# A hybrid decoder step on one core: the instruction planner's prices for VectorE, ScalarE and GpSimd are set to durations from the profile

## The chip, the cores and the metric

One core of a Trainium2 chip runs the whole program. Its engines are TensorE (PE, matmuls; PEld is its weight load), VectorE (DVE), ScalarE (ACT), GpSimd (POOL) and SyncE (SP, which starts most DMAs). The metric is device microseconds of one execution. The kernel before takes 2442.61 us, the median of 3 runs (2437.9 to 2442.79).

## The reference

One inference step of four layers on 1024 prompt positions and 8 x 4 sample positions, all with the same weights, width 1024, all in float32. Each layer is `x <- LayerNorm(ALPHA * x + mixer(x))`; the mixers are a short gated convolution (A), native sparse attention (B), an RG-LRU (C) and the convolution again (A).

```python
# A: short gated convolution
h, b_gate, c_gate, z = split(x @ w_in, 4)
y = (silu(z) * b_gate * causal_dwconv(c_gate * h, buf, conv_w)) @ w_out

# B: three attentions over one projection, added with gates, then (o * silu(z)) @ w_out
k_c, v_c = einsum('bnjcgd,cjgd->bncgd', blocks_of_32_rows, w_cmp)   # compressed rows of the cache
p_c = masked_softmax(q @ k_c)                                        # compressed attention
idx = top_k(sums of p_c by block of 64, 16)                          # selected blocks
o = g0 * (p_c @ v_c) + g1 * attend(q, rows of blocks idx) + g2 * attend(q, last 512 rows)

# C: gated linear recurrence along time
a = exp(-8 * softplus(-lam) * sigmoid(uc @ w_a + b_a))
b = sqrt(1 - a * a) * sigmoid(uc @ w_x + b_x) * uc
h[t] = a[t] * h[t-1] + b[t]
y = (silu(z) * h) @ w_out
```

The sample group attends to 4096 past rows in a paged cache, which is read through a page table. Outputs are both activations and the new states and caches.

## The kernel before

**Tiles and stages.** Activations lie transposed, channels on partitions, in 8 tiles of 128 channels by 1056 columns (1024 prompt, 32 sample). A dense product takes three blocks of 352 columns; every operand is split into a high and a low part, so a product over 1024 channels is 24 matmuls of 352 columns into one PSUM bank (`dense`). The high part is written by ACT (or DVE), the low part by DVE or POOL (`split`). The stages follow each other: layer A with the compression of the sample cache beside it (`layer_a`, `compress`, to 432 us), its output product and norm (`out_phase`), the projections of layer B (`b_project`), the sample group's attention (`decode`, 690 to 856), the prompt's attention (`prompt_attention`, to 1470), the norm of B, layer C (`layer_c`, 1590 to 1832), its norm, the second A (to 2325) and the last output product and norm (`final_phase`).

**The compression.** For each of 64 units (8 groups of rows by 8 sequences) POOL starts a gather of 1 MB from the cache, POOL or DVE (odd or even sequence) multiplies 1024 elements a partition by the weights, and DVE adds 512, 256 and 256 elements. A unit is recorded every 1/0.7 dense products (`RATE`), and a gather waits for the sum three units before (`GAHEAD`). The weights of a group have a single buffer.

**What sets the order.** Nothing is issued in the order in which it is written. `Rec` stands in place of the engines: each call is recorded as a step with its engine, a price in ns (`cost`, line 269), the tiles it reads and writes, and a due number, which is its place in the program less a shift (`AHEAD`, `DSH`: tables by kind of work). Up to six matmuls into one tile make one step. At the end of a part, `lay` simulates the five engines: at each turn the engine that can go first takes, of the steps that are ready by then, the one with the smallest due number. A step is ready when its producers have ended and a latency between the two engines has passed (`LAT`, line 246: 205 ns from PE to DVE, 192 from DVE to ACT, 141 from ACT to DVE, 127 from DVE to DVE), and when its buffers are free; buffers of a ring are given out in recorded order (`admit`). A change of ACT's table costs 1283 ns, a DMA takes its bytes at 360 a ns on a bus of its own plus 2000 ns. The simulated times are then thrown away: what is kept is the order of the steps on every engine. On the chip each engine runs its queue in that order and waits at its head for what is not there. Since nearly all calls go through `add`, the profile shows line 307 for them; line 312 is the gather.

The prompt's attention has a planner of its own (`Plan`), whose steps carry literal prices, and which does not call `cost`.

Of the kernel before, what the change touches and what calls it, by code (L numbers as in the profile page):

```python
# [240 lines left out]
class Rec:  # L241
# [27 lines left out]
    def cost(self, eng, name, a, k, out):  # L269
        def free(v):  # L270
            return int(np.prod(v.shape[1:]))
        n = free(out)
        if eng == "PE":
            if name == "transpose":
                return 109
            m = a[2]
            return max(free(m) / 2.27 * (4 if m.dtype == F32 else 1), 50) + 7
        if eng == "ACT":
            ap = sum(1 for x in (k.get("bias"), k.get("scale")) if x is not None and not isinstance(x, (int, float)))
            src = a[1]  # L280
            return n * .833 + 51 + (0 if isinstance(src, View) and src.t.whole else 43) + 93 * ap + (93 if k.get("accum_out") is not None else 0)
        if eng == "DVE":
            if name == "reciprocal":
                return 6.25 * n + 69
            if name == "tensor_tensor_scan":
                return n * 2.08 + 70
            if name in ("tensor_reduce", "max"):
                n = free(k["in_"])
            return n / .96 + 70
        if eng == "POOL":  # L290
            if name == "tensor_scalar":
                return .833 * n + 327
            if name in ("tensor_copy", "memset"):
                return .833 * n + 150
            return 2.1 * n + 150
        return 0

    def add(self, eng, real, name, a, k):
# [11 lines left out]
    def gather(self, out, src, idx, **keys):  # L310
        def fn():
            self.nc.gpsimd.indirect_dma_start(out=out.real(), out_offset=None, in_=src, in_offset=bass.IndirectOffsetOnAxis(ap=idx.real(), axis=0))
        self.record("POOL", "gather", 1040, fn, [out], [idx], out, **keys)

    def record(self, eng, name, cost, fn, outs, ins, out, rk=(), wk=(), a=(), k={}):
        last = self.ops[-1] if self.ops else None
        if eng == "PE" and last is not None and last.eng == "PE" and last.out is outs[0].t and len(last.fns) < 6 and last.due - self.pos + self.shift > -1.5:
            o = last
            o.cost += cost
            o.fns.append(fn)  # L320
        else:
            o = Step()
            o.eng, o.cost, o.due, o.fns, o.deps, o.tiles, o.takes, o.outs = eng, cost, self.pos - self.shift, [fn], set(), {}, [], []
            o.weak, o.follow = set(), []
            o.func = a[2] if eng == "ACT" and name == "activation" and a[2] in (AF.Tanh, AF.Exp, AF.Sqrt) else None
            o.out = outs[0].t if outs else None
            o.size = int(np.prod(out.shape)) * 4 if eng == "SP" or name == "gather" else 0
            self.pos += 1
            self.ops.append(o)
# [1908 lines left out]
class Plan:  # L2238
# [10 lines left out]
    def add(self, kind, eng, cost, due, fn, r=(), w=(), after=()):  # L2249
        n = len(self.ops)  # L2250
        deps = set(after)
        for k in r:
            if k in self.wr:
                deps.add(self.wr[k])
        for k in w:
            if k in self.wr:
                deps.add(self.wr[k])
            deps.update(self.rd.get(k, ()))
        for k in r:
            self.rd.setdefault(k, []).append(n)  # L2260
        for k in w:
            self.wr[k], self.rd[k] = n, []
        self.ops.append([eng, cost, due + self.off.get(kind, 0.0), fn, sorted(deps)])
        return n
# [155 lines left out]
```

## Time and profile before

| | |
|---|---|
| median of 3 runs | 2442.61 us |
| profiled execution | 2450.34 us |
| its span | 2448.6 us |
| mean granted TensorE clock | 0.971 |
| PE busy | 2318.3 us (95%) |
| DVE busy | 1594.0 us (65%) |
| ACT busy | 1206.7 us (49%) |
| POOL busy | 955.4 us (39%) |
| HBM traffic | 237.31 MB read, 84.48 MB written |

All times are of one profiled execution. An engine's busy time is the union of its instructions' recorded durations; a recorded duration can lie partly beside the next one's. Waits are put down to the semaphore that came last. PE is busy nearly all the time, so what matters of another engine is whether PE waits for it.

### The profile page before, as it was taken

The page shows a single profiled execution, that of the slowest core. Times are in us where ns is not written, and L with a number is a line of the kernel's source. Part 1 is how long each engine was busy: PE and PEld are TensorE (multiplying, and loading weights), DVE is VectorE, ACT ScalarE, POOL GpSimd, SP SyncE. Part 2 cuts the span into 40 slices and gives each one's busy share as a digit, 9 for nine tenths or more (in the row PEclk, how much of TensorE's full clock was granted, in tenths as well). Part 3 has the DMA queues.
Part 4 walks back from the last instruction along what each step waited for, and adds up shares of the span by engine and source line. Part 5 has one row for each costly group of instructions (what it writes and reads, how often), then busy time and mean ns, then how long its engine had stood idle before and what let it go on. Part 6 is the DMA issues. An engine that isn't in the chain of part 4 may idle for free. (4 is left out here: it accounts for less than half of the span.)

```text
span 2448.6 us, 41435 instructions
## 1 busy us (share of the span) xinstructions
PE 2318.3 (95%) x14801; PEld 2247.7 (92%) x14801; DVE 1594.0 (65%) x3686; ACT 1206.7 (49%) x2761; POOL 955.4 (39%) x1070
## 2 busy tenths in 40 slices
PE   8999997998989999999999999899989899999996
PEld 8999986997979889999999989899889899999996
DVE  5777865584368767777777766877873743333336
ACT  3211211244357778888888862568872432222233
POOL 3455543223148656656555542323452320000131
PEclk9999998999999999999999999999989999999998
DMA  8999987256367641111112314421204221111111
GB/s 286 352 340 350 341 273 235 90 188 219 93 204 259 249 133 50 51 35 46 43 45 68 121 44 150 137 80 44 60 26 127 83 66 52 44 41 55 35 45 71
DMA packets 334643, 320.35 MB, mean 131 GB/s; under 512 B 19462, under 2 KB 301542, under 8 KB 324964
## 3 DMA queue, kind: packets, MB, share of 16 engines
q1 hardware_dynamic: 325220, 250.58, 33.1%
q0 software_dynamic: 9216, 67.11, 7.2%
q8 instruction: 117, 1.92, 0.3%
q14 instruction: 90, 0.74, 0.1%
HBM read 237.31 MB, written 84.48 MB: 131 GB/s over the span
## 5 line engine op out<-in xcount | busy, mean ns | idle before, releaser
L307 PE MATMUL mm<-x,w 128*128 128x352 f32 x5760 | 947.9, 326 | 23.2 <-DVE c L307 9.9
L307 PEld LDWEIGHTS mm<-x,w 128*128 128x128 f32 x5760 | 937.8, 191 | 28.3 <-DVE c L307 10.4
L307 PE MATMUL mm<-big,w 128*128 128x352 f32 x2208 | 389.0, 331 | 9.9 <-ACT c L307 5.5
L307 PEld LDWEIGHTS mm<-big,w 128*128 128x128 f32 x2208 | 366.3, 193 | 13.7 <-ACT c L307 6.9
L307 POOL TENSOR_TENSOR w<-ws,w 128x1024 fp32r<-128x1024 f32 (+1 forms) x43 | 105.8, 2461 | 446.7 <-ACT w L307 426.8
L1965 DVE TENSOR_TENSOR c<-T,c 128x512 fp32r<-128x512 f32 (+1 forms) x320 | 204.8, 648 | 49.6 <-ACT c L1961 44.8
L1961 ACT CAST c<-T 128x512 fp32r<-128x512 f32 (+1 forms) x320 | 174.6, 552 | 59.5 <-PE T L1957 38.4
L307 ACT CAST w<-ws 128x1024 fp32r<-128x1024 f32 (+2 forms) x116 | 120.4, 1039 | 158.0 <-PE mm L307 122.9
L638 PE MATMUL D<-x,w 128*128 128x352 f32 x1008 | 195.4, 330 | 2.3 <-DVE big L2092 2.3
L1867 PE MATMUL A<-big 128*128 128x320 f32 (+11 forms) x832 | 181.8, 334 | 3.6 <-DVE ast L1892 1.8
L1972 PE MATMUL O<-c,big 128*128 128x256 f32 x1056 | 180.4, 291 | 0.5 <-ACT c L1961 0.2
L307 ACT CAST big<-aux 128x352 fp32r<-128x352 f32 (+3 forms) x116 | 45.7, 400 | 268.6 <-DVE aux L307 251.0
L307 DVE TENSOR_TENSOR big<-big 128x256 f32<-128x256 f32 (+3 forms) x204 | 145.9, 730 | 39.0 <-POOL big L307 35.0
L638 PEld LDWEIGHTS D<-x,w 128*128 128x128 f32 x1008 | 159.9, 188 | 5.7 <-DVE big L2092 3.5
L307 DVE TENSOR_TENSOR w<-ws,w 128x1024 fp32r<-128x1024 f32 (+2 forms) x73 | 90.9, 1245 | 110.2 <-ACT w L307 109.6
L307 POOL TENSOR_TENSOR big<-big,ws 128x1024 f32<-128x1024 f32 (+1 forms) x38 | 89.8, 2364 | 154.5 <-DMA big<-in_cache_nsa_kv,idx 69.8
L1972 PEld LDWEIGHTS O<-c,big 128*128 128x128 f32 x1056 | 147.2, 189 | 2.6 <-DVE c L1965 0.7
L1925 POOL TENSOR_SCALAR pr<-pr,G,ast 128x32 f32<-128x32 f32 (+6 forms) x192 | 126.4, 675 | 47.1 <-DVE ast L1936 42.3
L1867 PEld LDWEIGHTS A<-big 128*128 128x128 f32 x832 | 134.3, 192 | 10.4 <-PE A L1867 2.3
L307 DVE SCALAR_TENSOR_TENSOR c<-c,mm 128x352 f32<-128x352 f32 x125 | 64.3, 516 | 108.6 <-PE mm L307 53.9
L307 ACT ACTIVATE aux<-ws,PT 128x352 f32<-128x352 f32 (+2 forms) x72 | 42.6, 594 | 173.1 <-DVE ws L307 171.8
L1921 ACT ACTIVATE pr<-pr,ast 128x32 f32<-128x32 f32 (+6 forms) x192 | 118.4, 619 | 18.2 <-DVE ast L1892 17.1
(286 smaller groups left out, 4047.2 us busy)
## 6 DMA issues: line engine op xcount, KB each, us to landing
ws<-in_a_w_in SPq DMA_DIRECT2D x64, 512.0 KB
raw<-big SPq DMA_DIRECT2D x128, 256.0 KB
big<-raw SPq DMA_DIRECT2D x128, 256.0 KB
c<-dd SPq DMA_DIRECT2D x48, 176.0 KB
xs<-x SPq DMA_DIRECT2D x24, 352.0 KB
x<-xs SPq DMA_DIRECT2D x8, 1056.0 KB
ws<-in_a_w_out SPq DMA_DIRECT2D x16, 512.0 KB
ws<-in_c_w_in SPq DMA_DIRECT2D x16, 512.0 KB
```

What stands on the lines that cost most here:

```text
L307: getattr(real, name)(*[f(x) for x in a], **{q: f(x) for q, x in k.items()})
L638: self.nc.tensor.matmul(ps, a, b, start=n == 0, stop=n == 23 and last)
L1867: nc.tensor.matmul(o, q[:, hl, i * P:(i + 1) * P], k, start=m == 0, stop=m == 1)
L1921: nc.scalar.activation(S[:, a:a + m], S[:, a:a + m], AF.Exp, bias=st[:, k:k + 1], scale=-1.0, accum_out=st[:, 3 + k:4 + k])
L1925: nc.gpsimd.tensor_scalar(S[:, a:a + m], S[:, a:a + m], G[:, i, 16 * k + h:16 * k + h + 1], st[:, 6 + k:7 + k], op0=ALU.mult, op1=ALU.mult)
L1961: nc.scalar.copy(x["H"][:, 0:n], x["tp"][:, 0:n])
L1965: nc.vector.tensor_sub(x["L"][:, 0:n], x["tp"][:, 0:n], x["H"][:, 0:n].bitcast(F32))
L1972: nc.tensor.matmul(O, v, M[:, y * P:(y + 2) * P], start=done[0] == 0, stop=done[0] == total - 1)
```

## The change

Prices in `Rec.cost` and in `gather`. ACT: the fixed part goes from 51 to 160 ns, the addition for a source in SBUF from 43 to 35, for each per-partition operand from 93 to 100, for an accumulator from 93 to 185. DVE: the fixed part from 70 to 150 ns; the scan from 2.08 to 2.6 ns an element; an instruction with two tensor inputs of which none is in PSUM gets 1.4 ns an element and 130 ns. POOL: two-input instructions from 2.1 ns an element and 150 ns to 2.25 and 170. The gather from 1040 to 1130 ns. PE's prices, `LAT`, the DMA prices and all other tables stay.

```diff
--- before.py
+++ after.py
@@ -278,21 +278,24 @@
         if eng == "ACT":
             ap = sum(1 for x in (k.get("bias"), k.get("scale")) if x is not None and not isinstance(x, (int, float)))
             src = a[1]
-            return n * .833 + 51 + (0 if isinstance(src, View) and src.t.whole else 43) + 93 * ap + (93 if k.get("accum_out") is not None else 0)
+            return n * .833 + 160 + (0 if isinstance(src, View) and src.t.whole else 35) + 100 * ap + (185 if k.get("accum_out") is not None else 0)
         if eng == "DVE":
             if name == "reciprocal":
                 return 6.25 * n + 69
             if name == "tensor_tensor_scan":
-                return n * 2.08 + 70
+                return n * 2.6 + 150
             if name in ("tensor_reduce", "max"):
                 n = free(k["in_"])
-            return n / .96 + 70
+            ins = [x for x in a[1:] + [k.get("in0"), k.get("in1")] if isinstance(x, View) and free(x) > 1]
+            if len(ins) > 1 and not any(x.t.ring.tag in ("mm", "aux") for x in ins):
+                return n * 1.4 + 130
+            return n / .96 + 150
         if eng == "POOL":
             if name == "tensor_scalar":
                 return .833 * n + 327
             if name in ("tensor_copy", "memset"):
                 return .833 * n + 150
-            return 2.1 * n + 150
+            return 2.25 * n + 170
         return 0
 
     def add(self, eng, real, name, a, k):
@@ -310,7 +313,7 @@
     def gather(self, out, src, idx, **keys):
         def fn():
             self.nc.gpsimd.indirect_dma_start(out=out.real(), out_offset=None, in_=src, in_offset=bass.IndirectOffsetOnAxis(ap=idx.real(), axis=0))
-        self.record("POOL", "gather", 1040, fn, [out], [idx], out, **keys)
+        self.record("POOL", "gather", 1130, fn, [out], [idx], out, **keys)
 
     def record(self, eng, name, cost, fn, outs, ins, out, rk=(), wk=(), a=(), k={}):
         last = self.ops[-1] if self.ops else None
```

## Rows read from the trace of the kernel before

**Rows 1.** The page, part 1: busy us (share of the span) xinstructions of each engine
```profile
PE 2318.3 (95%) x14801; PEld 2247.7 (92%) x14801; DVE 1594.0 (65%) x3686; ACT 1206.7 (49%) x2761; POOL 955.4 (39%) x1070
```

**Rows 2.** Busy time by stage: stretch, us, PE PEld DVE ACT POOL, PEclk, DMA
```profile
0.00:432.00 432.00, 394.76 (x2392) 387.12 (x2393) 298.76 (x495) 88.22 (x162) 194.08 (x117) 0.97 0.93 311
...
690.00:856.00 166.00, 153.34 (x1037) 137.43 (x1038) 132.50 (x331) 119.57 (x227) 116.67 (x106) 0.95 0.70 239
856.00:1470.00 614.00, 601.84 (x4309) 580.54 (x4308) 462.37 (x1425) 495.15 (x1412) 347.96 (x590) 0.98 0.22 64
...
1590.00:1832.00 242.00, 222.20 (x1342) 218.73 (x1343) 191.88 (x350) 185.38 (x313) 94.55 (x84) 0.97 0.18 52
...
1955.00:2325.00 370.00, 369.57 (x2283) 369.60 (x2284) 139.38 (x279) 86.89 (x153) 27.37 (x19) 0.99 0.18 51
```

**Rows 3.** PE's waits, 432:690 (9), 690:856, 1470:1955 (20), 2325:2449: us, times, longest
```profile
PE mm L307 <- ACT c L307: 5.3, 1, 5.3
...
PE aux L307 <- POOL c L307: 0.2, 1, 0.2
...
PE aux L307 <- DMA sel<-kcd: 8.1, 1, 8.1
...
PE aux L307 <- DVE SC L307: 7.8, 1, 7.8
...
PE mm L307 <- DVE w L307: 1.0, 1, 1.0
...
PE aux L307 <- DVE c L307: 4.6, 4, 2.4
```

**Rows 4.** Timeline of PE, four stretches of 0:432: start, us, [idle before <-releaser]
```profile
328.06 2.42 PE L307 MATMUL mm<-x,w 128*128 128x352 f32 x7 [6.01 <-DVE c L307]
...
372.73 1.53 PE L307 MATMUL mm<-x,w 128*128 128x352 f32 x6 [3.84 <-DVE c L307]
...
400.92 1.54 PE L307 MATMUL mm<-x,w 128*128 128x352 f32 x4 [3.25 <-DVE ws L307]
...
429.80 1.02 PE L307 MATMUL aux<-idf,SC 128*18 128x128 f32 x4 [11.34 <-DVE big L307]
```

**Rows 5.** Timeline of DVE ahead of those four waits
```profile
320.66 1.22 DVE L307 TENSOR_TENSOR big<-big,ws 128x1024 f32<-128x1024 f32 x1 [8.41 <-DMA ws<-in_b_w_cmp]
...
371.01 1.23 DVE L307 TENSOR_TENSOR big<-big,ws 128x1024 f32<-128x1024 f32 x1 [7.83 <-DMA ws<-in_b_w_cmp]
...
394.31 3.80 DVE L307 TENSOR_TENSOR big<-big 128x512 f32<-128x512 f32 x3 [8.34 <-POOL big L307]
...
423.67 2.81 DVE L307 TENSOR_TENSOR big<-big 128x512 f32<-128x512 f32 x1 [7.11 <-POOL big L307]
```

**Rows 6.** Timeline of 1503.5:1505: a chain DVE, ACT, DVE in a norm stage
```profile
1503.60 0.50 DVE L307 SCALAR_TENSOR_TENSOR c<-c,mm 128x352 f32<-128x352 f32 x1
...
1504.19 0.50 ACT L307 ACTIVATE c<-c 128x352 f32<-128x352 f32 x1 [1.34 <-DVE c L307]
...
1504.72 0.80 DVE L307 TENSOR_TENSOR big<-big,c 128x352 f32<-128x352 f32 x1 [0.61 <-ACT c L307]
```

**Rows 7.** Timeline of DVE, 1575:1577: six instructions that don't wait for each other
```profile
1575.27 1.26 DVE L307 TENSOR_SCALAR c<-idf,stat 128x128 f32<-128x128 f32 x6
```

**Rows 8.** Groups by shape: line engine op xcount | busy us, mean ns | idle before
```profile
L307 DVE SCALAR_TENSOR_TENSOR c<-c,mm 128x352 f32<-128x352 f32 x125 | 64.3, 516 | 108.6 <-PE mm L307 53.9 <-ACT c L307 52.4 <-issue 1.0
...
L312 POOL DMA_INDIRECT big<-in_cache_nsa_kv,idx x64 | 74.8, 1169 | 80.5 <-DVE idx L307 16.6 <-DMA raw<-big 16.5 <-DVE c L307 15.0
...
L307 DVE TENSOR_TENSOR big<-big 128x512 f32<-128x512 f32 x66 | 64.6, 980 | 36.2 <-POOL big L307 35.0 <-DMA ws<-in_a_w_in 1.0
...
L307 DVE TENSOR_TENSOR c<-c 128x352 f32<-128x352 f32 x77 | 50.7, 703 | 8.2 <-ACT c L307 8.2
...
L307 ACT COPY c<-mm 128x352 f32<-128x352 f32 x48 | 21.3, 455 | 34.2 <-PE mm L307 34.2
...
L307 POOL TENSOR_TENSOR c<-c 128x352 f32<-128x352 f32 x19 | 20.8, 1095 | 50.1 <-DVE c L307 22.6 <-ACT c L307 10.7 <-issue 8.8
...
L307 DVE TENSOR_SCALAR c<-idf,stat 128x128 f32<-128x128 f32 x54 | 11.8, 281 | 0.0
```

## The prediction

> **What bounds the kernel now.** I read five views in this order. The page first: TensorE (PE) is busy for 2318.3 us of a span of 2448.6 [rows 1], so about 130 us are all that any new order of instructions could return. The profiled execution took 2450.34 us; the median of the three runs shown is 2442.61, 0.3% less. I make the sum in differences and add them to the median; on the profiled execution the same differences stand.
>
> Then the busy time by stage [rows 2]. In the second short-convolution layer (1955 to 2325) PE is busy for 369.57 of 370 us: nothing to win, only to lose. In the prompt attention (856 to 1470) it is idle for 12.2 us, and that stage is ordered by `Plan`, which carries its own prices; the diff does not touch them. Attention is a quarter of the time and stays as it is, but for its start. What the change can move is the first layer with the cache compression beside it (0 to 432: PE idle 37.2 us), the decode attention (690 to 856: 12.7), the RG-LRU layer (1590 to 1832: 19.8), the norm stages between them and the tail.
>
> Then who ended PE's waits [rows 3], then the four long waits of the first layer one by one [rows 4], and what VectorE (DVE) did in them [rows 5]. Last come the durations themselves: a dependent chain of three instructions [rows 6], a burst of independent ones [rows 7], and the means of the groups that the new prices stand for [rows 8].
>
> **The change, part by part.** No instruction is added, removed or altered. Only numbers in `Rec.cost` and `gather` change, and these decide at which simulated moment an instruction is ready and its engine free; `lay` then takes the ready one with the smallest due number. Every queue is affected at once: ACT, DVE and POOL directly, PE in how it interleaves, the DMA starts by when buffers come free.
>
> *The size of the prices.* DVE with one operand in PSUM, 352 wide: 352/.96+70 = 437 ns before, 517 after; the trace says 516. DVE with two SBUF inputs: 437 before, 623 after, trace 703; for 512: 603 before, 847 after, trace 980. ACT copying 352 from PSUM: 344 before, 453 after, trace 455. POOL on two SBUF inputs: 889 before, 962 after, trace 1095. Gather: 1040 before, 1130 after, trace 1169 [rows 8]. So the change does what it says: the new prices are recorded durations, still short for POOL and SBUF pairs.
>
> *Durations are not occupancies.* Six independent tensor_scalars, 281 ns each by their group [rows 8], took 1.26 us together [rows 7]: (1.26-0.281)/5 = 196 ns from start to start. The old price is 128/.96+70 = 203, the new 283. The last 85 ns of a recorded duration lie beside the next instruction. The same tail is in `LAT`, which is left alone: in the chain of rows 6 the DVE instruction starts at 1503.60 and the ACT instruction that needs it at 1504.19, 0.59 us later; the old plan says 437+192 = 629 ns, the new one 517+192 = 709. From ACT to the next DVE instruction it is 0.53 us; old 293+51+43+141 = 528, new 293+160+35+141 = 629. So old prices and `LAT` fit a chain through PSUM and ACT, and the new plan believes each such hop 80 to 100 ns too long. Where two SBUF inputs meet, it is the other way: there the old plan is short by a third and the new one nearly right. I expect both errors to matter, in different stages.
>
> The Trainium skill has a rule against my reading of the burst: VectorE: DVE Perf Modes, section The DRAIN you can't avoid, says that the next instruction does not start until the pipe is empty. By it duration would be occupancy, the new prices would be right throughout, and my loss below would go. The trace disagrees (196 ns apart at 281 ns each), and the same section says that an instruction that is not held starts earlier.
>
> *First term, the first layer: a gain.* The four waits of rows 4 are 6.01, 3.84, 3.25 and 11.34 us, 24.4 together. Rows 5 show why: DVE stands for 7 to 8 us at the head of its queue before a product or a sum of the compression, and that stands behind a load or behind POOL, while the dense work that frees PE's banks is queued behind it. The plan had believed the compression ready some 8 us too early. With the new prices it becomes ready later in the plan: by 90 (gather) + 174 (POOL product of 1024) = 0.26 us for an odd unit, by 90+427+244+302 = 1.06 us through the product and the three sums of an even one. The lateness that the plan does not know is in the DMA, whose price stays. I take 0.75 us, between the two and nearer to the even unit since both share DVE: 4 x 0.75 = 3 us gained. Bounds: nothing, and all 24.4 us, if the sums fall wholly behind the dense work. Off the front, the weight copies on ACT and the low parts on POOL are next, but PE sits behind neither there.
>
> *Second term, the norm stages and the RG-LRU layer: a loss.* Outside the first layer, decode and attention the views count 9 + 20 + 4 = 33 waits of PE on another engine [rows 3]. Their chains are of the kind of rows 6. Three hops are believed 0.08+0.10+0.08 = 0.26 us later than they are, and a chain with a reduction or a square root has more; then the plan places one more independent instruction (0.44 us of DVE, by 516 less the 80 overlapped) in front in three of four cases: 0.33 us a wait, 33 x 0.33 = 11 us. Bounds: one SBUF-pair instruction of 0.70 us before each, 23 us; and below nothing, 11 us gained, if the better price of the SBUF pairs moves as many out of the way. What is queued behind the displaced instruction is the rest of its own chain, and PE behind that.
>
> *Third term, decode.* DVE is busy for 132.5 of 166 us, ACT 119.6, POOL 116.7, and PE 153.3 [rows 2]. PE is hardly held there, so the old order costs little; I set 0, bounded by -5 (its 12.7 us of idle PE less the one wait of 8.1 us on a DMA [rows 3], which no price here moves) and +24.6 (36 units, each with one DVE instruction of 512 from PSUM, 512/.96+150 = 683 ns, in front of what PE needs).
>
> The three shape-dependent odds (the scan's slope, accumulators, ACT pointers) go into the second term. PE's own price is unchanged, and each dense product takes its bank in recorded order, so PE's order can only change between products and small matmuls.
>
> Sum: -3 + 11 + 0 = +8 us: 2442.6 + 8 = 2450.6, or 2450 in round numbers (2458 on the profiled execution).
>
> **Rivals.**
> *The compression moves behind the dense work (faster).* This is one mechanism, at DVE's queue in 0 to 432. For it: the new price of SBUF pairs is the biggest correction (437 to 623, 1137 to 1564 for a product), DVE is busy 298.8 of 432 us there [rows 2], and the old plan thinks it far emptier. Against it: the standing times are 7 to 8 us and the correction is 1. It decides from the point where a sum becomes ready in the plan after the dense instruction that is now queued behind it. Half of 24.4 us back and no loss elsewhere: 2442.6 - 12 = 2430.
> *The order is pinned (no change).* Buffers are given out in recorded order and due numbers stay, so instructions swap only where their engine has slack. For it: PE at 369.57 of 370 us in one stage and 394.8 of 432 in another [rows 2]. Against it: DVE's prices rise by 18 to 43%, far more than its slack of 31% in the first layer allows to hide. Time 2443.
> *Decode is disturbed (slower).* DVE and ACT are full for four fifths and seven tenths there, so an order that is worse by one instruction a unit reaches PE. Price 24.6 us: 2467. Against it: in 690 to 856 both neighbours of a displaced instruction are from the same unit.
> *Occupancy is duration.* Then the second term is 0: 2442.6 - 3 = 2440. Rows 7 speak against it. This is where the rule quoted above from the Trainium skill would lead.
>
> **How the numbers follow.** A measurement of this kernel tells about 0.2%, 5 us, from no change. Chances: forecast 0.37, compression 0.33, pinned 0.16, decode 0.10, occupancy 0.04. Slower by over 5 us: 0.30 of the forecast, decode's 0.10, 0.02 of pinned = 0.42. Faster by over 5 us: 0.30 of the compression and 0.02 each of pinned and occupancy = 0.34. The rest, 0.24, is within. Range: from 2424 (-19, most of the four waits back) to 2474 (+31, 23 of the second term and a third of decode's); the forecast alone, with its second term between 0 and 23, spans 2440 to 2463. The two signs are close, because one mechanism that I can name gains and one loses, and neither is measured before the run.
>
> **What would show it.** Right: PE idle in 0 to 432 falls by a few us only, with the four waits at about their length; PE idle in the norm stages and 1590 to 1832 grows by about 10; 1955 to 2325 and attention keep their length within 1 or 2 us. Wrong by the first rival: the waits near 322, 369, 398 and 418 shrink to half, the compression's last sum comes after the dense work's last, and the norm stages stay. Wrong by the second: all stages within 2 us. Decode: 690 to 856 grows by over 10 us and PE waits for DVE inside units. Groups' mean durations should not move, but for SBUF pairs of DVE that now meet POOL more or less often; if those move by over 50 ns, contention and not order made the difference, and my working is wrong in kind.

## The result, and the profile after

The kernel after takes 2427.52 us, the median of 6 runs (2423.55 to 2430.12); the kernel before, beside it, 2442.7 (6 runs). The ratio is 0.994, with an interval of 0.9925 to 0.9956: 15 us faster. The forecast was 2450, slower. The time lies in the range, the direction is wrong.

The page of after, part 1, answers to [rows 1]. PE runs the same number of matmuls and is busy for 12.7 us less; ACT has four instructions fewer, which are table loads (below).

```profile
PE 2305.6 (95%) x14801; PEld 2234.8 (92%) x14801; DVE 1583.6 (65%) x3686; ACT 1203.7 (50%) x2757; POOL 959.3 (40%) x1070
```

Busy time by stage, after; columns as in [rows 2]. The cuts lie where the same work ends.

```profile
0.00:430.00 430.00, 394.09 (x2396) 386.21 (x2397) 302.42 (x497) 88.09 (x161) 194.20 (x117) 0.98 0.93 311
430.00:572.00 142.00, 133.12 (x796) 130.64 (x795) 90.96 (x184) 49.60 (x90) 37.00 (x32) 0.94 0.45 148
572.00:696.00 124.00, 113.65 (x607) 98.53 (x607) 43.95 (x136) 48.72 (x124) 25.86 (x34) 0.94 0.45 143
696.00:860.00 164.00, 150.56 (x1032) 134.43 (x1032) 131.07 (x330) 121.00 (x228) 118.45 (x106) 0.97 0.72 242
860.00:1474.00 614.00, 601.68 (x4312) 580.44 (x4312) 462.40 (x1424) 494.49 (x1412) 346.72 (x590) 0.99 0.22 65
...
1590.00:1820.30 230.30, 222.12 (x1341) 220.12 (x1340) 176.11 (x336) 176.51 (x302) 96.54 (x83) 0.97 0.20 59
1820.30:1930.00 109.70, 109.53 (x694) 108.54 (x693) 67.47 (x130) 39.88 (x70) 36.55 (x29) 1.00 0.36 111
```

Two stages of before that the rows ahead of the prediction don't hold, in the same view:

```profile
575.00:690.00 115.00, 111.20 (x605) 96.80 (x603) 37.66 (x126) 43.41 (x111) 22.18 (x30) 0.99 0.43 136
...
1832.00:1955.00 123.00, 116.17 (x694) 114.90 (x694) 71.97 (x128) 42.64 (x76) 42.27 (x32) 0.94 0.33 101
```

Layer C and its output stage got shorter: 1341 matmuls in 230.3 us against 1342 in 242.0, then 694 in 109.70 against 694 in 123.00. The second half of layer B's projections got longer: 607 matmuls in 124 us, against 605 in 115. Attention is the same.

To compare kernels I cut each trace at the same matmuls (the first of a product, the first of attention, and so on) and take the lengths. One stage needs care: the first layer differs between executions of one order. In eleven kernels that plan it alike its profiled length runs from 421.8 to 433.7 us, and the profiled execution of before (2450.34 against the median 2442.61) is a long one. Later stages of one order repeat within about 2 us, decode within about 5. So the column "first layer" has the profiled length plus what the median differs from the profiled time; in the eleven kernels it then stays between -3.9 and +3.2 of before. This correction is an assumption, not a reading, and it is large where the profiled execution was an extreme one.

| kernel (new prices where) | median us | ratio to before (interval) | first layer | its output and norm | B proj. | norm of B | C | out of C, norm |
|---|---|---|---|---|---|---|---|---|
| before | 2442.7 | | 424.8 | 107.5 | 141.9 | 92.6 | 269.4 | 112.9 |
| after (all) | 2427.5 | .994 (.9925-.9956) | +7.0 | -3.3 | +13.9 | -3.7 | -12.0 | -9.2 |
| e1 last part | 2413.0 | .9883 (.9862-.9904) | +0.8 | +1.3 | -1.0 | -3.7 | -13.9 | -8.7 |
| e2 first part | 2461.8 | 1.0088 (1.0071-1.0106) | +7.9 | -2.1 | +12.6 | 0 | +2.4 | 0 |
| f1 last, DVE | 2411.8 | .9865 (.9847-.9883) | -0.4 | -0.1 | +0.1 | -3.9 | -16.5 | -5.5 |
| f2 last, ACT+POOL | 2428.9 | .9927 (.9901-.9953) | -3.2 | +1.4 | +0.7 | +1.8 | -10.5 | -2.5 |
| f3 last, DVE pairs only | 2423.5 | .991 (.9888-.9932) | -3.9 | +1.9 | -0.2 | -3.0 | -4.4 | -3.4 |
| h1 first layer, its norm | 2456.8 | 1.0057 (1.0038-1.0076) | +6.5 | -2.9 | +9.2 | +1.7 | +1.3 | -0.8 |
| h3 first part, DVE+POOL | 2455.2 | 1.005 (1.0035-1.0065) | +5.4 | -2.3 | +7.7 | +0.2 | +2.4 | 0 |
| i2 first part, DVE | 2447.1 | 1.0016 (1.0001-1.0031) | -0.2 | -1.9 | +5.3 | +1.7 | +1.3 | -0.7 |
| i1 as h3, DVE less 80 ns | 2452.2 | 1.0044 (1.0028-1.0059) | +10.7 | -0.8 | +2.0 | +2.2 | +1.3 | -0.7 |

"Norm of B" runs to the first product of C, "C" to the first matmul of its output product. "Last part" is the planned part from the norm of B to the end, "first part" the first layer, its norm and B's projections; decode is the part between. So the change is a gain of some 29 us behind attention and a loss of some 18 ahead of it: with the last part alone the kernel takes 2413 us, with the first alone 2462.

**Where the gain is.** The norm of B first. PE in before, then DVE and POOL in before, then PE and DVE in after:

```profile
1540.12 3.05 PE L307 MATMUL mm<-big,w 128*128 128x352 f32 x18
1544.55 0.38 PE L307 MATMUL aux<-ones_m,big 128*128 128x1 f32 x2 [1.38 <-POOL big L307]
1545.37 1.28 PE L307 MATMUL aux<-ones_m,big 128*128 128x1 f32 x10 [0.44 <-DVE big L307]
1546.51 1.20 PE L307 MATMUL mm<-big,w 128*128 128x352 f32 x6
```

```profile
1542.66 1.05 DVE L307 TENSOR_TENSOR x<-c,x 128x352 fp32r<-128x352 f32 x1
1543.64 1.24 DVE L307 TENSOR_TENSOR x<-ws,x 128x352 fp32r<-128x352 f32 x1
1544.80 0.51 DVE L307 TENSOR_TENSOR big<-big,c 128x352 f32<-128x352 f32 x1
...
1543.28 1.21 POOL L307 TENSOR_TENSOR big<-big,ws 128x352 f32<-128x352 f32 x1
```

```profile
1543.98 4.01 PE L310 MATMUL mm<-big,w 128*128 128x352 f32 x24
1547.83 1.39 PE L310 MATMUL aux<-ones_m,big 128*128 128x1 f32 x12
```

```profile
1541.67 0.52 DVE L310 TENSOR_TENSOR x<-c,x 128x352 fp32r<-128x352 f32 x1
1542.11 0.52 DVE L310 TENSOR_TENSOR big<-big,ws 128x352 f32<-128x352 f32 x1
1542.54 0.52 DVE L310 TENSOR_TENSOR big<-big,c 128x352 f32<-128x352 f32 x1
...
1546.24 1.26 DVE L310 TENSOR_TENSOR big<-big,c 128x352 f32<-128x352 f32 x1
```

Before, the plan holds a 352-wide SBUF pair for 437 ns and cuts a dense product after 18 matmuls to place the column sums of `big`; on the chip PE stands 1.38 us for POOL's sum into `big`, which ends at 1544.49, and 0.44 us for DVE's, which is queued behind pairs that take 1.05 and 1.24 us. After, the column sums come behind a whole product and wait for nothing.

Then the end of layer C. PE and SyncE's queue in before, then in after:

```profile
1823.25 0.93 PE L307 MATMUL aux<-idf,SC 128*36 128x128 f32 x7
1831.97 0.40 PE L307 MATMUL aux<-idf,SC 128*36 128x128 f32 x1 [7.80 <-DVE SC L307]
```

```profile
1754.78 17.60 SPq L307 DMA_DIRECT2D ws<-in_c_w_out  x3
1822.80 0.43 SPq L307 DMA_DIRECT2D ws<-in_c_w_out  x1
1831.92 0.37 SPq L307 DMA_DIRECT2D ws<-in_c_w_out  x1
```

```profile
1746.43 0.60 PE L310 MATMUL aux<-idf,SC 128*36 128x128 f32 x4
...
1831.88 0.60 PE L310 MATMUL aux<-idf,SC 128*36 128x128 f32 x4
```

```profile
1756.59 59.53 SPq L310 DMA_DIRECT2D ws<-in_c_w_out  x6
```

`put_rows` turns the new states round with eight transposes. In before all eight stand in front of the output product, and the last waits 7.80 us for the final state. In after the first four run 77 us earlier (at 1746.43 instead of 1823.25), the output product starts, and the last four stand inside it. Their buffer `rows` is taken from the ring `ws` ahead of the output weights, so these load earlier too: six loads go out from 1756.59, where in before three go and the fourth leaves at 1822.80.

This end of the layer, from its last product on `x` to the first matmul of the output product, takes 8.9 us in before and 0.2 in after, so it is 8.8 of the 12.0 us that layer C gains; the other 3.2 lie further inside the layer, and no run shows what makes them.

One rival can be settled. The new order also needs fewer loads of ACT's tables (before, then after):

```profile
L307 ACT ACT_TABLE_LOAD x46 | 59.0, 1283 | 8.4 <-DVE c L307 4.9 <-PE mm L307 2.1 <-PEq L2405 0.7
...
L310 ACT ACT_TABLE_LOAD x42 | 53.9, 1283 | 4.5 <-PE mm L310 2.1 <-DVE c L310 1.1 <-PEq L2408 0.7
```

They don't make the gain: f1 has 46 of them like before, and its layer C is 16.5 us shorter; e3 has 42 like after, and its layer C gains 0.4.

**Where the loss is.** Layer B's projections, PE in before, PE in after, DVE in after, ACT in after:

```profile
573.80 5.43 PE L307 MATMUL mm<-w,x 128*128 128x384 f32 x18 [5.34 <-ACT c L307]
```

```profile
544.35 0.44 PE L310 MATMUL mm<-big,x 128*128 128x384 f32 x1 [1.66 <-ACT x L310]
545.95 2.93 PE L310 MATMUL mm<-big,x 128*128 128x384 f32 x8 [1.16 <-POOL x L310]
...
553.19 2.29 PE L310 MATMUL aux<-ones_m,big 128*128 128x1 f32 x10 [4.10 <-DVE big L310]
...
580.11 2.29 PE L310 MATMUL mm<-w,x 128*128 128x384 f32 x6 [8.67 <-ACT c L310]
```

```profile
548.87 1.09 DVE L310 TENSOR_TENSOR c<-c 128x352 f32<-128x352 f32 x2 [2.17 <-DMA c<-dd]
...
552.62 0.51 DVE L310 TENSOR_TENSOR big<-big,c 128x352 f32<-128x352 f32 x1
```

```profile
578.63 1.04 ACT L310 CAST big<-ws 128x1024 fp32r<-128x1024 f32 x1 [2.58 <-DMA ws<-in_b_w_in]
579.58 0.47 ACT L310 COPY c<-mm 128x384 f32<-128x384 f32 x1
```

PE enters a product whose `x` the norm of the first layer has not written (1.66, 1.16 us), stands 4.10 us for a sum that is queued on DVE behind a step that waits for a transfer, and 8.67 us for the copy that empties its bank, which stands on ACT behind a weight cast that waits for its load. Over the whole of these projections PE is idle for 18.8 us, where before has 9.2. The idle time is only part of the loss: in the second stretch the granted clock is 0.94 where before had 0.99.

### The profile page after: what moved, and what is told of

It reads as the page before. It is cut to its first block, busy times and chain, and to the rows that moved or that the text cites. A ratio compares the mean times of both kernels' runs of the same rounds, so it can differ in the third digit from the quotient of the medians.

```text
span 2423.7 us, 41400 instructions
## 1 busy us (share of the span) xinstructions
PE 2305.6 (95%) x14801; PEld 2234.8 (92%) x14801; DVE 1583.6 (65%) x3686; ACT 1203.7 (50%) x2757; POOL 959.3 (40%) x1070
## 5 line engine op out<-in xcount | busy, mean ns | idle before, releaser
L310 PE MATMUL mm<-big,w 128*128 128x352 f32 x2208 | 375.4, 325 | 1.0 <-ACT c L310 1.0
L310 PEld LDWEIGHTS mm<-big,w 128*128 128x128 f32 x2208 | 357.2, 189 | 2.8 <-ACT c L310 1.3
```

The source lines that it names most:

```text
L310: getattr(real, name)(*[f(x) for x in a], **{q: f(x) for q, x in k.items()})
```

## The experiments

Most kernels hold both price functions, old (`was`) and new (`told`); the set `fresh` names the engines whose new prices hold for what is recorded from there on:

```diff
+    def cost(self, eng, name, a, k, out):
+        return (self.told if eng in self.fresh else self.was)(eng, name, a, k, out)
```

**e1: the last part alone, e2: the first part alone.**

```diff
+        k.rec.fresh = frozenset(("DVE", "ACT", "POOL"))    # e1: ahead of the part behind attention
...
+                    k.rec.fresh = frozenset(("DVE", "ACT", "POOL"))    # e2: ahead of the first layer; empty from decode on
```

> The new prices in the last planned part alone (norm of B, layer C, its norm, the second A, the tail); the parts before it keep the old ones. By stages the two profiles differ by about -29 us there and by +4 us before it. Theory L (the higher prices make the plan believe results late, so that PE's short steps which need them are queued behind dense products, above all in layer C and its norm): the last part keeps its whole gain, so the time is 2442.7 minus 18 to 29, 2414 to 2425, below that of the full change (2427.5). Rival: the last part gains because it is entered in another state (later start, other buffers), then most of it goes, 2435 to 2443.

> The new prices in the first planned part alone (first layer with the compression, its norm, projections of B). If the parts add up, +8 us: 2448 to 2453, with the first layer about 5 us shorter and the projections about 14 us longer. Rival (the compression's order is the gain, as the prediction's first rival had it): 2430 or less.

Measured 2413.03 and 2461.83. The change is two changes with opposite signs: e1 keeps the gain and e2 the loss, each in the stages in which after has it. e2 lies above the 2448 to 2453 expected, which counted on a first layer 5 us shorter; by the corrected length it is 7.9 longer.

**e3: old prices, with the shared tails in the latency; e4: new slopes without the tails.** The tail is the part of a recorded duration that lies beside the next instruction. e3 believes every result 100 (ACT), 80 (DVE) or 40 ns (POOL) later, but engines free as before. e4 keeps the new slopes and takes the tails out.

```diff
-           ("DVE", "ACT"): 192, ("DVE", "PE"): 275,
+           ("DVE", "ACT"): 272, ("DVE", "PE"): 355,       # e3, and the other pairs alike
...
-                return n * 1.4 + 130
+                return n * 1.4 + 50                        # e4
-            return n / .96 + 150
+            return n / .96 + 70                            # e4; scan + 70, POOL + 130, ACT and the gather as before
```

> Old prices everywhere, but each latency of the plan that starts at ACT is 100 ns longer, at DVE 80, at POOL 40: results are believed late by the same tails, while the engines' loads stay as they were believed before. Theory L: at least half of the change's gain comes back, 2425 to 2436. Rival O (what helps is that the loads are right: pairs of SBUF operands and POOL are believed busy for as long as they are): no gain, 2440 to 2447.

> Prices by occupancy: the new slopes (pairs of SBUF operands 1.4 ns an element, scan 2.6, POOL 2.25) with the fixed parts less the tail that overlaps (DVE 70 and 50, POOL 130, ACT as before, gather as before). Theory L: little gain, since what is added is load and not lateness, 2436 to 2446, but for chains through SBUF pairs. Rival O: the gain of the full change or more, 2420 to 2430.

e3: 2449.93, ratio 1.0045 (1.0027 to 1.0062), slower, with C at -0.4 and its output stage at -2.4: to believe results later earns next to nothing of the gain. e4: 2429.87, 0.9955 (0.9941 to 0.9969), with C at -12.2, the output stage at -6.6 and the projections at -0.1: a plan that holds the engines longer gains, and without the tails the loss in B is not there. But layer C gains in another place than in after, since the end of the layer is as it was:

```profile
1811.37 0.40 PE L310 MATMUL aux<-idf,SC 128*36 128x128 f32 x1 [7.40 <-DVE SC L310]
```

The end takes 8.5 us of 8.9, and 11.8 us are gained ahead of it, where after gains 3.2. So the nearly equal lengths of C in the two kernels have different causes, and what e4's is stays open. In both, the first layer is longer by 15 us if corrected as above. For these two that is not shown: their profiled executions were the fastest of each kernel (2432.9 and 2421.51), and uncorrected the layer takes 422.8 and 431.2 us, no longer than in before (432.5).

**f1 to f3: the last part by engine and term.**

```diff
+        k.rec.fresh = frozenset(("DVE",))           # f1
+        k.rec.fresh = frozenset(("ACT", "POOL"))    # f2
...
+            if len(ins) > 1 and not any(x.t.ring.tag in ("mm", "aux") for x in ins):
+                return n * 1.4 + 50                 # f3: the only new price, last part
```

> In the last planned part alone, the new prices of VectorE alone. The stages of the runs so far put about 26 us of gain there (norm of B -4, layer C -12 to -14, its norm -7 to -9), and longer latencies alone gave none of it. Theory O (VectorE's load was believed too small): nearly the whole of it, 2413 to 2422. Rival A (the load of ScalarE and GpSimd decides in layer C, where ACT is busy for 185 of 242 us): under a third of it, 2434 to 2443.

> The counterpart: in the last part alone, the new prices of ScalarE and GpSimd alone. Theory O: under a third of the 26 us, 2434 to 2443, and PE's wait of 7.8 us at the end of layer C stays. Rival A: most of it, 2413 to 2422.

> In the last part alone, one price alone: VectorE's instructions with two SBUF operands at 1.4 ns an element plus 50 (their occupancy); no fixed part, no scan, nothing else. If the pairs are the load that was missing, at least two thirds of what VectorE's new prices give together: 2413 to 2426. If it is the scan or the fixed part of the many small instructions, under a third: 2434 to 2443.

2411.77, 2428.92 and 2423.54. DVE alone brings all, and the pairs' price alone 19 us of it, with the norm of B at -3.0, near after's -3.7. ACT's and POOL's prices bring the end of layer C (0.2 us instead of 8.9; C at -10.5) and not the norm (+1.8); f2's time lies between its two cases. With DVE's prices the end takes 2.3 us and 9.8 are gained ahead of it; with the pairs' alone the end is as in before (9.3). 31 and 14 us don't add: e1 has both and 30 us. What no run tests is a shift of the prices that has no reason: e3 is the only other order here that was not meant to correct an engine's load, and it gained nothing in C, but how often any new order would gain as much is not known.

**f4 and g3: the state rows by hand.** Old prices; f4 moves the second four transposes' due number back by 40, g3 the first four forward by 150.

```diff
+            if n == 36 and h:
+                self.rec.shift = -40      # f4
+            if n == 36 and not h:
+                self.rec.shift = 150      # g3
             for k in range(4):
```

> Old prices everywhere; only the second four small transposes at the end of layer C, behind which PE stood for 7.8 us, get a due number 40 places later, so that they are queued behind the first dense products of the next stage. If this one place of PE's queue is most of layer C's gain: layer C 7 to 9 us shorter, 2433 to 2437. If the wait only moves (the dense product needs the same late result): 2440 to 2445.

> Old prices everywhere; the first four transposes of layer C's state rows and their copy get a due number 150 products earlier, so that on PE they stand two gate products before the end of the layer and not in front of the output product. Theory W (the 9 to 12 us at the end of layer C come from the buffer of these rows, which stands in the ring ahead of the output product's weights): the weights load earlier, the wait of 7.8 us goes, layer C is 7 to 11 us shorter, total 2432 to 2436. Rival (the wait is only the visible end of a DVE queue that runs late, and goes elsewhere when the transposes move): layer C within 3 us of before, total 2440 to 2445.

f4 tested nothing: 2443.95, and the transposes stayed where they were with the wait of 7.8 us, presumably because a step's readiness decides there, not its due number; no run shows that. g3 did move them, and only the steps around them: 2437.62, ratio 0.9979 (0.9963 to 0.9996). PE and SyncE in g3:

```profile
1775.78 0.84 PE L307 MATMUL aux<-idf,SC 128*36 128x128 f32 x4
1825.77 0.49 PE L307 MATMUL aux<-idf,SC 128*36 128x128 f32 x3
1827.47 0.40 PE L307 MATMUL aux<-idf,SC 128*36 128x128 f32 x1 [1.21 <-DVE SC L307]
```

```profile
1746.14 66.35 SPq L307 DMA_DIRECT2D ws<-in_c_w_out  x6
```

The wait of 7.80 us is 1.21, the six loads leave in one row as in after, and the output product starts 0.2 us behind the last product on `x`, as in after. The mechanism of the end is shown, at 8.8 us. C as a whole is only 5.8 us shorter, since the part ahead of the end is 3.0 longer, and its output stage is 1.2 longer: 5 us of the total, under the 7 to 11 expected of C.

**g4: f1 and g3 together, the best version.**

> DVE's new prices in the last planned part alone (2411.8 us when run by itself), and the first four transposes of the state rows 150 products earlier as well. If the two gains are one and the same buffer: 2410 to 2414. If the half of the end-of-layer gain that DVE's prices alone left (layer C lost 9.6 us by that place with ACT's, 4.7 with DVE's) is still there to take: 2405 to 2409, with the out-product starting 4 to 5 us earlier.

2404.38, ratio 0.9844 (0.9825 to 0.9864): a little better than the better of the two cases. It beats after by 23 us. Its norm of B is at -3.9, C at -18.2, the output stage at -9.3.

**g1, g2, h2: new prices in layer B's own steps alone (ACT; DVE and POOL; all three).**

```diff
+                            k.rec.fresh = frozenset(("ACT",))         # g1; ("DVE", "POOL"): g2; all three: h2
                             B = k.layer_b(pm, X, bs, ds)
```

> Old prices everywhere, but ACT's new ones in the projections of layer B. With all three engines' new prices the stage from 572 us on took about 13 us longer than before. Theory A (ACT's longer prices make the plan place the weight cast and norm work ahead of the copy that empties PE's bank): the projections lose 10 to 14 us, total 2453 to 2457, and PE waits over 5 us for ACT's copy of c there. Theory D (the loss is DVE's, by its fixed part or its pairs): the projections stay within 2 us, total 2441 to 2445.

> Old prices everywhere, but DVE's and POOL's new ones in the projections of layer B. Theory A (the loss of 13 us there is ACT's): the projections stay within 2 us, total 2441 to 2445. Theory D (it is DVE's or POOL's): they lose 10 to 14 us, total 2453 to 2457. If neither run of the two loses, it takes both prices together.

> Old prices everywhere, new ones of all three engines in layer B's own steps. If it takes ACT's and DVE's together there: the projections lose 10 to 14 us, total 2451 to 2458. If the norm's prices are needed: within 3 us, total 2441 to 2446.

2444.75, 2443.89, 2440.12; ratios 1.0002, 1.0, 0.9989, all with an interval across 1. The projections stay within 1 us. Both theories of g1 and g2 fall: new prices in B's own steps alone don't make the loss.

**h1, h3, i2, i1: the norm in front of them.** h1: all new prices in the first layer and its norm, none in B. h3: DVE's and POOL's in the whole first part. i2: DVE's alone. i1: as h3, with each of DVE's prices 80 ns shorter.

```diff
+                    k.rec.fresh = frozenset(("DVE", "ACT", "POOL")) # h1, ahead of the first layer
+                    k.rec.fresh = frozenset(("DVE", "POOL"))        # h3, i1; ("DVE",): i2
...
-                return n * 1.4 + 130
+                return n * 1.4 + 50                                 # i1, and / .96 + 70, scan + 70
```

> New prices in the first layer and the norm behind it, old ones in layer B's own steps. If the loss of 13 us in the projections is set by the norm's chain (its steps placed otherwise, and SyncE's queue, which carries the norm's transfers and B's weight loads in one line, with them): the projections lose 10 to 14 us, total 2451 to 2458. If by layer B's own steps: within 3 us, total 2438 to 2445.

> New prices of DVE and POOL in the whole first planned part (first layer, norm, projections), ACT's old. If ACT's price takes part in the loss: the projections within 3 us, total 2438 to 2445. If DVE's fixed part or slope makes it by itself: they lose 10 to 14 us, total 2451 to 2458.

> New prices of DVE alone in the whole first planned part, all else old. If DVE's 80 ns make the loss: the projections lose 6 to 10 us, total 2450 to 2457. If POOL's price or the gather's is needed: within 3 us, total 2440 to 2446.

> New prices of DVE and POOL in the whole first planned part, but each of DVE's 80 ns less (1.4 ns an element and 50 for SBUF pairs, the old 70 elsewhere, the scan 2.6 and 70); ACT old. With the 80 ns in, this run took 2455.2 us and the projections lost 7.7. If the shared 80 ns make the loss: the projections within 3 us, total 2440 to 2446. If the slope for SBUF pairs, POOL's 20 to 60 ns or the gather's 90 make it: they lose 6 to 10 us again, total 2450 to 2457.

h1 loses 9.2 us in the projections without one new price in them: the order of the norm makes it. DVE's prices alone lose 5.3, with POOL's 7.7, and 2.0 once DVE's 80 ns are out. So DVE's tail makes the larger part of h3's loss. With all prices in the norm it is 9.2 (h1), with new prices in B's own steps on top of that 12.6 (e2). i1's total is 2452, above its 2440 to 2446, since its first layer is 10.7 us longer by the corrected length; i2, with DVE's prices alone, has that layer at -0.2, and its loss of 5.3 and its total (2447.14) fall between the two cases.

**h4: as e2, but the plan believes B's weight loads 3 us later.**

```diff
-                o.end = bus + 2000
+                o.end = bus + 2000 + o.slow     # 3000 for B's weights, else 0
```

> All new prices in the first planned part, as in the run that took 2461.8 us, and the plan believes the loads of layer B's weights 3 us later than it does. If the place of the loss is the cast that waits for a load in front of the copies on ACT: the copies come first, PE's wait of 8 us there goes, the projections lose under 5 us, total 2445 to 2452. If the loads are late because SyncE's queue stands behind the norm's transfers, whatever the plan thinks of the load: still 10 us or more lost, total 2455 to 2465.

2457.16, 1.0057 (1.0041 to 1.0073). The projections lose 6.8 where e2 lost 12.6, between the two expectations, and the wait behind ACT grows from 8.0 to 9.2 us. PE in h4:

```profile
580.60 6.07 PE L344 MATMUL mm<-w,x 128*128 128x384 f32 x24 [9.23 <-ACT c L344]
```

So the cast in front of the copy, the longest wait in after, is not the cause: e4 has the same wait at 7.7 us and no loss. What differs is what comes before it, the waits for `x` and `big`: the wait for the sum, 3.95 us in e2, is 0.45 in h4 and does not show in e4.

## Why the prediction was wrong

**The second term failed.** It put 33 waits at 0.33 us each, because "the new plan believes each such hop 80 to 100 ns too long". In the stages of 24 of them it measured -3.7 (norm of B), -12.0 (C), -9.2 (its output) and -0.8 (tail), 25.7 us gained; with the other nine, below, it is 15.1 gained, outside its lower bound of 11 gained. The bound's own words named part of what happened ("if the better price of the SBUF pairs moves as many out of the way"): that price alone gains 19 us in the last part (f3). The end of layer C is another part, and f2 has it without that price. I weighed two errors by the number of waits. They don't have equal size: one wait at the end of C was 7.8 us long and went as a whole, and the clock went down with the waits. In 1832 to 1955 before has 6.8 us of idle PE and a granted clock of 0.94; after has 0.2 and 1.00 for the same 694 matmuls. Of 13.3 us, half is idle time and half is clock.

**Its mechanism acted in one place.** Over the 9 waits of 432 to 690 after loses 13.9 - 3.3 = 10.6 us, and i1 against h3 shows that DVE's 80 ns make most of it (5.7 of 7.7 us) where DVE's and POOL's prices alone are new. But e3, which believes results later by those tails and holds no engine longer, does not lose there (+1.4). So the loss there comes not from "each hop too long" but from the engine believed held too long, which places other steps ahead.

**The first term probably had the wrong sign.** Forecast -3. In the two profiled executions the layer is 2.8 us shorter (432.5 and 429.7), but before's was a long one. With the correction the four kernels with all new prices there (after, e2, h1, h4) have it at +7.0, +7.9, +6.5 and +11.4; without it they take 429.7 to 438.9 us, 433.5 in the mean, where the eleven with old prices take 427.2 in the mean. PE's waits in 0 to 432 of after:

```profile
PE aux L310 <- DVE big L310: 14.1, 2, 12.3
PE mm L310 <- DVE ws L310: 10.3, 4, 4.5
```

The longest is 12.3 us where it was 11.34 [rows 4]. The waits of 6.01 and 3.84 us are gone or under 1 us, but others are new, up to 4.5 us. So the first rival, the compression moving behind the dense work, came close with its time (2430) by luck: its gain was to lie in this layer, and it lies behind attention. Which price lengthens this layer is open: DVE's alone do not (i2), and of e3 and e4 only the corrected lengths (+15.1, +14.9) say so.

**The third term and the rest.** Decode was set at 0; it is 3.0 us shorter in after, within what same-priced kernels vary. Attention (-0.8) stayed. The second A layer is 3.2 us shorter, a little outside the 1 to 2 us I gave. "Order is pinned" fell.

**Groups' means.** I wrote that a group moving by over 50 ns would make my working wrong in kind. Several did, both ways (980 before [rows 8] for the second; 546 before for the first), and not in the compression alone:

```profile
L310 DVE TENSOR_TENSOR big<-big 128x256 f32<-128x256 f32 x120 | 78.3, 668 | 0.7
...
L310 DVE TENSOR_TENSOR big<-big 128x512 f32<-128x512 f32 x66 | 56.7, 867 | 20.4 <-POOL big L310 20.3
...
L307 DVE TENSOR_TENSOR x<-c,x 128x352 fp32r<-128x352 f32 x32 | 23.6, 748 | 0.3 <-ACT x L307 0.3
...
L310 DVE TENSOR_TENSOR x<-c,x 128x352 fp32r<-128x352 f32 x32 | 18.8, 596 | 0.9 <-ACT x L310 0.9
```

The two sums of the compression together cost DVE 135.0 us where they cost 129.3; the norms' pairs went from 748 to 596 ns. DVE's group with one operand in PSUM holds (515 for 516). So order changes durations, which my sum left out. How much of the gain or the loss is made by these changed durations, and how much by the order itself, no run separates.

**Occupancy is duration.** The rival drawn from the Trainium skill (VectorE: DVE Perf Modes, The DRAIN you can't avoid) gave 2440. After's own pairs start 0.44 us apart at 0.52 us each (1541.67, 1542.11, 1542.54 above), and taking the shared 80 ns out of the plan (i1) removed 5.7 of 7.7 us in the projections. This trace speaks against the rule here; the rival's time came nearer than mine, by a different way.

## What to carry to other kernels

A recorded duration and the time for which an instruction holds its engine (start to start) are two things, and a planner needs to know which of them its price is. A price that fits the profile better does not by itself give a better order: the pairs' price gained 19 us behind attention (f3), and the same slope ahead of it, with POOL's prices, cost about 9 (i1); the shared tail made most of h3's loss in layer B's projections, and yet f1, with the tails and the scan's new price, did better behind attention than f3 without them. So try a change of prices on each planned part by itself: here one part gained 30 us, another lost 19, and the sum hid both. Size a wait by its own length and by the clock behind it, not by a mean over a count.

## What the runs showed of the hardware

A long wait of PE cost more than its length here. Before's PE stands from 1823 to 1832, and the next 10 us run at a granted clock of 0.71, with PE busy for all 10 (columns as in [rows 2]):

```profile
1823.00:1832.00 9.00, 1.20 (x11) 0.80 (x10) 8.65 (x16) 7.31 (x10) 4.17 (x4) 0.75 0.34 98
1832.00:1842.00 10.00, 10.00 (x45) 9.79 (x46) 5.54 (x5) 2.40 (x4) 3.28 (x2) 0.71 0.62 175
1842.00:1852.00 10.00, 10.00 (x61) 9.57 (x60) 3.46 (x4) 2.83 (x5) 2.39 (x1) 1.00 0.28 90
```

0.71 lies between the two levels, 2.4 GHz (1.00) and 1.2 GHz (0.50): it is 5.8 of 10 us at the lower. 45 matmuls run in these ten microseconds and 61 in the next: 16 fewer, by estimate 2.6 us more on a wait of 7.8. One execution is one sample: behind the same wait (6.9 to 8.1 us) the 10 us have a granted clock of 0.73 in e3, 0.74 in f3, 0.78 in f4 and 0.83 in e4.

An SBUF pair of one shape takes 0.52 or about 1.26 us on DVE (1542.54 and 1546.24 above): no single price is right for it, and the new 623 ns lie between the two cases. The Trainium skill (SBUF — State Buffer, SBUF: two separate sides) tells of a lock between DVE's instructions with two SBUF inputs and GpSimd's that read SBUF, where the later one blocks; the long pair here lies beside two POOL instructions that fill 1545.90 to 1548.30. No run here took the neighbour away.
